# Remainders of the first mixer by VectorE, buffers of transposing streams in turn, and token weights at one byte offset, in a two-layer decoder kernel

## The chip, the cores and the metric

One core of a Trainium2 chip runs the kernel. The metric is device time in microseconds (us) of one execution, as the median of several runs. The engines are named as in the profile: PE is TensorE, PEld its weight loads, DVE is VectorE, ACT is ScalarE, POOL is GpSimd, SP is SyncE, which issues DMAs.

## The reference, cut to what matters

The kernel computes two decoder layers for 256 tokens of 1024 float32 channels, with a root-mean-square norm before each part and at the end. Layer 0 mixes with a gated delta rule (8 heads of 64) beside a short gated convolution; layer 1 with sparse attention. Each layer has a squared-ReLU MLP of 4096 hidden channels.

```python
def reference(x, ...):
    for layer in range(DEPTH):
        h = rms_norm(x, mix_norm[layer])
        if layer % 2 == 0:
            x = x + gdn_shortconv_mixer(h, ...)
        else:
            x = x + nsa_mixer(h, ...)
        x = x + squared_relu_mlp(rms_norm(x, mlp_norm[layer]), w_up[layer], w_down[layer])
    return rms_norm(x, final_norm)

def gdn_shortconv_mixer(h, ...):
    qkv, z, a, b, b_gate, c_gate, hs = jnp.split(h @ w_in, ..., axis=-1)
    qkv = jax.nn.silu(causal_dwconv(qkv, qkv_conv))
    g = -jnp.exp(a_log) * jax.nn.softplus(a + dt_bias)
    o = gated_delta_rule_chunked(l2_normalize(q), l2_normalize(k), v, g, jax.nn.sigmoid(b))
    o = rms_norm(o, o_norm) * jax.nn.silu(z)
    y_b = b_gate * causal_dwconv(c_gate * hs, sc_conv)
    return jnp.concatenate([o, y_b], axis=-1) @ w_out
```

The delta rule solves unit lower-triangular systems of 64 x 64 for every chunk of 64 tokens and every head.

## The kernel before, in words

**Weights in units.** All weights lie in one DRAM tensor, `wts`. SP loads them in pieces of 512 KB into eight staging slots, `st` (128 partitions x 1024 float32), as slots come free. Each 128 x 1024 piece is a *unit*, with a running number `i`. `splits` (L508) makes two halves of each unit: `uh`, which ACT writes as a rounded copy, and the remainder `ul = st - uh`. Four buffers of each hold them in turn (`uh0` to `uh3`, `ul0` to `ul3`). The remainder is made in one of two ways. For most units DVE subtracts (`V.tensor_sub`). For units in the tuple `BYDMA` (L37) ACT writes -uh into `ul`, and `refill` (L529) has POOL issue a DMA that adds `st` to it.

**Products.** A projection multiplies each block by `mm256`, three PE matmuls: high weights by high activations (`xh`), high weights by low activations (`xl`), and remainder by high activations. So PE needs a unit's `uh` for two matmuls and its `ul` for the third. Where activations stand still and weights move, in the projections of one result per token (`proj_tok` and `proj_tok2`, units of 528 and 560 columns instead of 1024), a unit's two halves of 264 or 280 columns are taken one after the other out of `uh` and `ul`.

**What the units are.** 0 to 7 the first projection (k), 8 to 15 the per-token projection of z, a and b (528 columns), 16 to 19 v, 20 to 23 q, 24 to 27 the gate Cg, 28 to 31 h and 32 to 35 Bg of the convolution, 36 to 43 the output projection of the mixer (its products of `yb`, the convolution's result, come before those of `ya`, the delta rule's), 44 to 107 the first MLP. Layer 1 has 108 to 139 (120 to 127 the second per-token projection, 560 columns) and its MLP 140 to 203.

**The first mixer.** `layer0` (L993) computes beside the projections the norms of k and q (`lsq`, which PE sums over partitions by a matmul with `par`), the decay (`g`), the products of keys in a chunk (`al`), and their triangular inverse in `invert`: eight alternating groups of 64 matmuls of 32 x 32 on PE, `left` from `al` and `tt`, `right` from `uc` and `ys`, with a step of DVE between two of them that makes the next `ys`, or the next `tt` and its transpose `uc`. Then come the chain over the chunks, the output `o`, its four transposes on PE (`par,o`), and `ya`. The short convolution (`prepool`, `cvpool`, `tap`, `CG`) is on DVE and POOL.

**Layer 1.** `combine` spawns four `turn` streams for each pair of heads; each takes a PSUM bank and then one of four buffers `pts`, transposes on PE and copies out.

**What sets the order.** The kernel's parts are Python generators. A planner (class `Order`, L166) keeps the time of every engine by a cost table, and at every `yield` decides which stream issues next: streams wait for flags (`yield 'flag'`), take tokens out of counted stocks (`yield 'take'`, `give`) and have priorities. So the program has a fixed order on each engine, and any changed cost or wait can move instructions of all of them. All are recorded in one helper and show line L329 in the profile; tiles tell them apart.

Of the kernel before, what the change touches and what calls it, by code (L numbers as in the profile page):

```python
# [10 lines left out]
F32 = mybir.dt.float32  # L11
F32R = mybir.dt.float32r
BF16 = mybir.dt.bfloat16
I32 = mybir.dt.int32
AF = mybir.ActivationFunctionType
# [11 lines left out]
UN = 1024  # L27
# [6 lines left out]
KPOOL, VPOOL, QPOOL, CVB = (), (), (0, 1, 2, 3), {'conv': 4, 'pool': 2}  # L34
TAP = {'V': 290}
CHAIN, EARLY, TOK_FIRST = 0, 16, False
BYDMA, DLAT = (*range(20, 44, 2), *range(113, 121, 2), *range(129, 141, 2)), 4500  # L37
YIELD = (0.0, 0.0, 0.0)
TICK, BUSY = 10240 / 3, 1500.0
FULL, DRAIN, BARE, STAY, LEAVE = (128, 128), 0.0, 0.0, 0.0, 0.0  # L40
# [1 line left out]
MAIN, SPLIT, SHARE, LIMIT, FLOOR, CAP, SPARE = 9, 0.5, 0.5, 300, -1500.0, 4000.0, 1  # L42
# [123 lines left out]
class Order:  # L166
# [21 lines left out]
    def spawn(self, gen, prio=None):  # L188
        c = self.cur
        if prio is None:  # L190
            prio = 1 if c is None or c.prio in (MAIN, SPLIT) else c.prio
        s = Stream(gen, prio, c)
        self.streams.append(s)
        self._next(s, None)
# [11 lines left out]
    def give(self, name):  # L206
        self.tokens[name].append(self._now())
# [174 lines left out]


BANK = ('bank',)
UB, SB, SPARE1 = 4, 8, 0
SLOTS, PTS = 4, 4
SQ0, NA0 = 'A', dict(V=334)
# [22 lines left out]
def _build(ctx, nc, tc, wts, xin, parin, out, off):  # L410
    e = Ctx()
    order = e.order = Order(8)
    V, A, PE, G = e.eng = [Timed(order, n, x) for n, x in (('V', nc.vector), ('A', nc.scalar), ('PE', nc.tensor),
                                                           ('G', nc.gpsimd))]
# [5 lines left out]
    unitp = pool("unit")  # L420
# [90 lines left out]
    def splits(first):  # L511
        for i in range(first, len(units), 2):
            p, o, n = units[i]
            order.cur.prio = 0 if i < EARLY else SPLIT
            if i >= UB:
                yield 'flag', f'ud{i - UB}'
            yield 'flag', f'ld{p}'
            src = staged[p][:, o:o + n]

            hi = unitp.tile([128, UN + 64], F32R, name=f"uh{i % UB}", tag=f"uh{i % UB}")[:, 32:32 + UN]  # L520
            lo = unitp.tile([128, UN + 64], F32R, name=f"ul{i % UB}")[:, :UN]
            yield 'A'
            A.activation(hi[:, :n], src, AF.Copy)
            made[i] = hi, lo
            if i in BYDMA:
                yield 'A'
                A.activation(lo[:, :n], hi[:, :n].bitcast(F32), AF.Copy, scale=-1.0)
                spawn(refill(i, lo[:, :n], src), SPLIT)
            else:  # L529
                yield 'V'  # L530
                V.tensor_sub(lo[:, :n], src, hi[:, :n].bitcast(F32))
                split_done(i)

    def refill(i, lo, src):
        yield 'G'
        G.dma_start(lo.bitcast(F32), src, accum_op=OP.add)
        order.later(DLAT)
        split_done(i)
# [120 lines left out]
    def proj_tok(norm, half, finish, prio=None):  # L659

        accs = yield from banks(4)
        for k in range(KT):
            hi, lo = yield from unit()
            yield 'flag', f'n{norm.idx}x{k}'
            for t in range(2):
                xt = norm.x[:, k, :, t * 128:t * 128 + 128]
                for b in range(2):
                    if b % GT == 0:
                        yield 'PE'
                    s = slice(b * half, b * half + half)  # L670
                    mm256(accs[2 * t + b][:, :half], xt[:, 0], xt[:, 1], hi[:, s], lo[:, s], k == 0, k == KT - 1)
        spawn(finish(accs), prio)

    def proj_tok2(norm, half, finish):

        for b in range(2):
            accs = yield from banks(2)
            for k in range(KT):
                if k % 2 == 0:
                    hi, lo = yield from unit()  # L680
                yield 'flag', f'n{norm.idx}x{k}'
                s = slice(k % 2 * half, k % 2 * half + half)
                for t in range(2):
                    yield 'PE'
                    xt = norm.x[:, k, :, t * 128:t * 128 + 128]
                    mm256(accs[t][:, :half], xt[:, 0], xt[:, 1], hi[:, s], lo[:, s], k == 0, k == KT - 1)
            spawn(finish(accs, b))
# [878 lines left out]
def layer1(e, n, nxt):  # L1566
# [4 lines left out]
    with ExitStack() as ctx:  # L1571
# [368 lines left out]
        def combine(i, p, PX):  # L1940
            u = 2 * i + p
            yield 'flag', f'pw{u}.0'
            if not MERGE:
                ob = yield BANK
                O = ob[:, :T]
            turns, spreads, ts4 = [4], [2], {}
            for b in range(2):
                yield 'flag', f'pw{u}.{b}'
                tss = ts4[b] = [None, None]
                for s in range(2):  # L1950
                    spawn(turn(u, b, s, PX, tss, turns), TURN)
                if not MERGE:
                    spawn(spread(i, p, b, tss, O, spreads))
            if MERGE:
                for b in range(2):
                    for s in range(2):
                        yield 'flag', f'ts{u}.{b}{s}'
                ob = yield BANK
                O = ob[:, :T]
                yield SMALL  # L1960
                for b in range(2):
                    products(p, b, ts4[b], O, not b)
            else:
                yield 'flag', f'pv{u}'
            yield 'flag', 'cmp1'
            yield 'flag', f'pct{i}'
            yield 'PE'
            pct, left = pcts[i]
            if CL:
                x = pct.rearrange("p a t q -> p a (t q)")  # L1970
                e.mm256(O, *VCB2[p], x[:, 0], x[:, 1], False, True)
            else:
                PE.matmul(O, VCB2[p], pct.rearrange("p t q -> p (t q)"), start=False, stop=True)
            left[0] -= 1
            if not left[0]:
                give('pct')
            if ohl[i] is None:
                ohl[i] = p1.tile([128, 2, 2, T], F32R, name=f"ohl{i}", tag=f"ohl{i}")
            yield from hilo(ohl[i][:, 0, p], ohl[i][:, 1, p], O)
            release(ob)  # L1980
            flag(f'o{u}')

        def turn(u, b, s, PX, tss, left):
            tb = yield BANK
            tp = tb[:, :384]
            yield 'take', 'pts', PTS
            yield 'PE'
            e.keep(tb)
            PE.transpose(tp[:, :128], PX[0][:, s, b], ident)
            PE.transpose(tp[:, 128:256], PX[1][:, s, b, :128], ident)  # L1990
            PE.transpose(tp[:, 256:], PX[1][:, s, b, 128:], ident)
            left[0] -= 1
            if not left[0]:
                give(f'slot{u % SLOTS}')
            ts = p2.tile([128, 384], F32, name="pts", tag="pts", bufs=PTS)
            yield from copy(ts, tp, 'V' if s else 'A')
            release(tb)
            tss[s] = ts
            flag(f'ts{u}.{b}{s}')
# [83 lines left out]
```

## Time and profile before

| | |
|---|---|
| time, median of 3 runs | 672.96 us (672.41 to 673.91) |
| time of the profiled execution | 674.54 us |
| its span | 672.7 us |
| mean granted TensorE clock | 0.988 |
| busy PE, DVE, ACT, POOL | 97%, 68%, 58%, 20% of the span |
| DMA, mean | 179 GB/s |

The profile is of one execution. Its span reaches from the first instruction to the last; the execution's own time is 1.8 us longer. PE's busy share is an average over stages: in the first mixer and in the attention PE waits, in the MLPs it does not. The granted clock is a share of full speed: 1.00 is the upper of two levels (2.4 GHz), 0.50 the lower (1.2 GHz).

### The profile page before, as it was taken

Reading aid. Unit: us, or ns where it says so; the run is one execution under the profiler, and the core shown is the slowest. Engines: PE = TensorE matmul, PEld = TensorE weight load, DVE = VectorE, ACT = ScalarE, POOL = GpSimd, SP = SyncE. Lnnn points to the kernel's source line nnn. Section 1 sums busy time; section 2 is a strip of 40 time slices with the busy share of each in tenths; the row PEclk is TensorE's granted clock in tenths of the full one; section 3 lists DMA queues with packets and bytes.
Section 4 is the critical chain, followed back from the end, with each engine's and each line's share of the span. In section 5 each row is a group of like instructions: output and inputs, shape, how many; then the busy total and the mean of one; then the engine's idle time right before and its main releaser. Section 6 shows DMA issues by size and latency. Waiting matters only on the chain.

```text
span 672.7 us, 16231 instructions
## 1 busy us (share of the span) xinstructions
PE 650.2 (97%) x6642; PEld 623.5 (93%) x6644; DVE 460.4 (68%) x899; ACT 387.7 (58%) x727; POOL 134.4 (20%) x179
## 2 busy tenths in 40 slices
PE   8999789999999999999999999999999999999995
PEld 5999679988999999999999886898999999999995
DVE  6998445865887776555566898897678777644441
ACT  7577234445676665434446679898567666434430
POOL 1012765611300000012024352120220000012121
PEclk9999789999999999999999999999999999999999
DMA  8884654556666666666666748653555555555401
GB/s 293 301 211 157 174 147 120 140 150 154 222 186 190 193 192 196 198 193 190 193 189 160 223 158 291 185 128 89 170 206 188 189 195 200 197 191 189 158 1 63
DMA packets 35642, 120.62 MB, mean 179 GB/s; under 512 B 4080, under 2 KB 4592, under 8 KB 35568
## 3 DMA queue, kind: packets, MB, share of 16 engines
q1 hardware_dynamic: 32112, 107.66, 49.1%
q0 software_dynamic: 3168, 11.54, 9.0%
q8 instruction: 52, 0.85, 0.5%
q10 hardware_dynamic: 288, 0.39, 0.2%
q14 instruction: 22, 0.18, 0.1%
HBM read 106.99 MB, written 1.05 MB: 161 GB/s over the span
## 4 chain that ended last, share of the span: by engine, by line
PE 80%; DVE 9%; ACT 4%; issue 3%; DMA 2%; SPq 0%; DVEq 0%; ACTq 0%
PE b L329 80%; DVE ul L329 2%; ACT uh L329 1%; DMA ul<-st 1%; DMA X<-xt 1%; DMA st<-wts 1%; DVE cvconv L329 1%; DVE rqt L329 1%; ACT E L329 1%; ACT ul L329 1%; DVE al L329 1%; DVE lc L329 0%; DVE u L329 0%; DVE tt L329 0%; DVE nacc L329 0%
## 5 line engine op out<-in xcount | busy, mean ns | idle before, releaser
L329 ACT ACTIVATE uh<-st 128x1024 fp32r<-128x1024 f32 (+3 forms) x204 | 206.2, 1012 | 218.4 <-PE b L329 187.5
L329 PE MATMUL b<-x,uh 128*128 128x256 f32 x1664 | 295.6, 282 | 2.0 <-ACT uh L329 1.8
L329 DVE TENSOR_TENSOR ul<-st,uh 128x1024 fp32r<-128x1024 f32 (+3 forms) x182 | 213.9, 1177 | 119.2 <-ACT uh L329 118.9
L329 PEld LDWEIGHTS b<-x,uh 128*128 128x128 f32 x1664 | 254.2, 190 | 4.1 <-ACT uh L329 1.7
L329 PE MATMUL b<-x,ul 128*128 128x256 f32 x832 | 233.1, 280 | 2.5 <-DVE ul L329 1.3
L329 PE MATMUL b<-U,uh 128*128 128x256 f32 x1024 | 174.2, 276 | 0.0
L329 PEld LDWEIGHTS b<-x,ul 128*128 128x128 f32 x832 | 158.2, 190 | 4.0 <-DVE ul L329 2.6
L329 PEld LDWEIGHTS b<-U,uh 128*128 128x128 f32 x1024 | 154.1, 188 | 0.0
L329 PE MATMUL b<-U,ul 128*128 128x256 f32 x512 | 141.3, 276 | 0.0
L329 PEld LDWEIGHTS b<-U,ul 128*128 128x128 f32 x512 | 96.1, 188 | 0.0
L329 POOL TENSOR_TENSOR nacc<-nacc,sq 128x256 f32<-128x256 f32 x24 | 32.4, 1348 | 227.1 <-ACT sq L329 217.4
L329 POOL DMA_DIRECT2D ul<-st x22 | 19.3, 876 | 80.4 <-ACT ul L329 36.4
L329 DVE SCALAR_TENSOR_TENSOR t<-b,rbc 128x256 f32<-128x256 f32 x64 | 26.6, 424 | 8.3 <-PE b L329 8.3
L329 ACT ACTIVATE U<-u 128x256 fp32r<-128x256 f32 x64 | 26.8, 419 | 2.0
L329 ACT ACTIVATE px<-b,nm 128x256 f32<-128x256 f32 (+1 forms) x64 | 26.3, 423 | 2.0 <-DVE nm L329 1.7
L329 DVE TENSOR_TENSOR U<-u,U 128x256 fp32r<-128x256 f32 x64 | 26.5, 419 | 0.0
L329 POOL TENSOR_TENSOR X<-X,par 128x256 f32<-128x256 f32 x8 | 5.6, 702 | 100.3 <-ACT nacc L329 91.7
L329 ACT ACTIVATE u<-t 128x256 f32<-128x256 f32 x64 | 25.6, 401 | 0.0
L329 DVE TENSOR_TENSOR X<-X,b 128x256 f32<-128x256 f32 (+1 forms) x28 | 13.9, 514 | 16.1 <-PE b L329 16.1
L329 PE MATMUL b<-uh,x 128*128 128x264 f32 (+1 forms) x128 | 24.5, 288 | 0.0
L329 PE MATMUL b<-ohl,uh 128*128 128x256 f32 x128 | 23.9, 287 | 0.2
L329 ACT ACTIVATE ul<-uh 128x1024 fp32r<-128x1024 f32 x22 | 23.2, 1057 | 0.4
(276 smaller groups left out, 793.9 us busy)
## 6 DMA issues: line engine op xcount, KB each, us to landing
st<-wts SPq DMA_DIRECT2D x188, 512.0 KB, 4.3
ul<-st POOLq DMA_DIRECT2D x22, 512.0 KB, 5.4
st<-wts SPq DMA_DIRECT2D x8, 280.0 KB, 3.2
st<-wts SPq DMA_DIRECT2D x8, 264.0 KB, 5.9
st<-wts SPq DMA_DIRECT2D x8, 256.0 KB, 6.1
X<-xt SPq DMA_DIRECT2D x3, 256.0 KB, 6.1
par<-par SPq DMA_DIRECT2D x1, 525.0 KB, 5.8
out_dram<-X SPq DMA_DIRECT2D x2, 256.0 KB, 2.7
```

The costliest lines, as they stand in the source:

```text
L329: r = f(*a, **k)
```

## The change

It has three parts. `BYDMA` shrinks from 22 units to 12: units 22, 24, ... 42 get their remainder from DVE in place of ACT, POOL and a DMA; unit 18 gets it from ACT, POOL and a DMA in place of DVE; unit 20 and those of layer 1 stay. In `combine` a token, of which there is one, is taken before the four `turn` streams are spawned and given back when the fourth has taken its `pts`; and a `turn` takes `pts` ahead of its bank. The per-token weights of 528 and 560 columns lie with their halves 320 elements apart, from element 16 on, in both `uh` and `ul`: each half begins at byte 64 of 256. Before, the halves of `uh` began at bytes 128 and 160 of 256 (264 columns) or 128 and 224 (280), those of `ul` at 0 and 32 or 0 and 96.

```diff
--- before.py
+++ after.py
@@ -34,7 +34,7 @@
 KPOOL, VPOOL, QPOOL, CVB = (), (), (0, 1, 2, 3), {'conv': 4, 'pool': 2}
 TAP = {'V': 290}
 CHAIN, EARLY, TOK_FIRST = 0, 16, False
-BYDMA, DLAT = (*range(20, 44, 2), *range(113, 121, 2), *range(129, 141, 2)), 4500
+BYDMA, DLAT = (18, 20, *range(113, 121, 2), *range(129, 141, 2)), 4500
 YIELD = (0.0, 0.0, 0.0)
 TICK, BUSY = 10240 / 3, 1500.0
 FULL, DRAIN, BARE, STAY, LEAVE = (128, 128), 0.0, 0.0, 0.0, 0.0
@@ -382,6 +382,7 @@
 
 
 BANK = ('bank',)
+TOK, STEP = (528, 560), 320
 UB, SB, SPARE1 = 4, 8, 0
 SLOTS, PTS = 4, 4
 SQ0, NA0 = 'A', dict(V=334)
@@ -517,18 +518,24 @@
             yield 'flag', f'ld{p}'
             src = staged[p][:, o:o + n]
 
-            hi = unitp.tile([128, UN + 64], F32R, name=f"uh{i % UB}", tag=f"uh{i % UB}")[:, 32:32 + UN]
-            lo = unitp.tile([128, UN + 64], F32R, name=f"ul{i % UB}")[:, :UN]
+            hi = unitp.tile([128, UN + 64], F32R, name=f"uh{i % UB}", tag=f"uh{i % UB}")
+            lo = unitp.tile([128, UN + 64], F32R, name=f"ul{i % UB}")
+            if n in TOK:
+
+                made[i] = parts = [a[:, 16:16 + 2 * STEP] for a in (hi, lo)]
+                hi, lo = (a.rearrange("p (b c) -> p b c", b=2)[:, :, :n // 2] for a in parts)
+                src = src.rearrange("p (b c) -> p b c", b=2)
+            else:
+                made[i] = hi, lo = hi[:, 32:32 + n], lo[:, :n]
             yield 'A'
-            A.activation(hi[:, :n], src, AF.Copy)
-            made[i] = hi, lo
+            A.activation(hi, src, AF.Copy)
             if i in BYDMA:
                 yield 'A'
-                A.activation(lo[:, :n], hi[:, :n].bitcast(F32), AF.Copy, scale=-1.0)
-                spawn(refill(i, lo[:, :n], src), SPLIT)
+                A.activation(lo, hi.bitcast(F32), AF.Copy, scale=-1.0)
+                spawn(refill(i, lo, src), SPLIT)
             else:
                 yield 'V'
-                V.tensor_sub(lo[:, :n], src, hi[:, :n].bitcast(F32))
+                V.tensor_sub(lo, src, hi.bitcast(F32))
                 split_done(i)
 
     def refill(i, lo, src):
@@ -667,7 +674,7 @@
                 for b in range(2):
                     if b % GT == 0:
                         yield 'PE'
-                    s = slice(b * half, b * half + half)
+                    s = slice(b * STEP, b * STEP + half)
                     mm256(accs[2 * t + b][:, :half], xt[:, 0], xt[:, 1], hi[:, s], lo[:, s], k == 0, k == KT - 1)
         spawn(finish(accs), prio)
 
@@ -679,7 +686,7 @@
                 if k % 2 == 0:
                     hi, lo = yield from unit()
                 yield 'flag', f'n{norm.idx}x{k}'
-                s = slice(k % 2 * half, k % 2 * half + half)
+                s = slice(k % 2 * STEP, k % 2 * STEP + half)
                 for t in range(2):
                     yield 'PE'
                     xt = norm.x[:, k, :, t * 128:t * 128 + 128]
@@ -1943,7 +1950,8 @@
             if not MERGE:
                 ob = yield BANK
                 O = ob[:, :T]
-            turns, spreads, ts4 = [4], [2], {}
+            turns, spreads, ts4 = [4, 4], [2], {}
+            yield 'take', 'turns', 1
             for b in range(2):
                 yield 'flag', f'pw{u}.{b}'
                 tss = ts4[b] = [None, None]
@@ -1981,9 +1989,12 @@
             flag(f'o{u}')
 
         def turn(u, b, s, PX, tss, left):
+            yield 'take', 'pts', PTS
+            left[1] -= 1
+            if not left[1]:
+                give('turns')
             tb = yield BANK
             tp = tb[:, :384]
-            yield 'take', 'pts', PTS
             yield 'PE'
             e.keep(tb)
             PE.transpose(tp[:, :128], PX[0][:, s, b], ident)
```

The planner then writes another order in the first mixer. PE has the same 5762 matmul instructions in both orders.

ACT, where the v projection begins; `uh2` and `ul2` here are of unit 18, `uh3` of unit 19, `uh0` of unit 20. Before:

```order
L329 ACTIVATE uh2_552<-st_420 128x1024
L329 ACTIVATE K_89<-cvconv_509 128x256
L329 ACTIVATE uh3_581<-st_440 128x1024
L329 ACTIVATE lsq_602<-K_89 128x256
L329 ACTIVATE uh0_611<-st_462 128x1024
L329 ACTIVATE ul0_612<-uh0_611 128x1024
```

and now:

```order
L329 ACTIVATE uh2_552<-st_420 128x1024
L329 ACTIVATE K_89<-cvconv_509 128x256
L329 ACTIVATE ul2_553<-uh2_552 128x1024
L329 ACTIVATE uh3_582<-st_440 128x1024
L329 ACTIVATE lsq_616<-K_89 128x256
L329 ACTIVATE gz0_604<-b7_368,ncol_333 128x256
```

The negation `ul2` of unit 18 stands ahead of the copy of unit 19, and unit 20's copy and negation come later.

DVE, in the triangular inverse, from the first transpose `uc1` to the first `ys`. Before:

```order
L329 STREAM_TRANSPOSE uc1_990<-tt1_988 128x256
L329 TENSOR_TENSOR bv1_1051<-b2_895,beta_98 128x512
L329 TENSOR_TENSOR prepool0_106<-b5_849,rbc_375 128x256
L329 TENSOR_TENSOR prepool1_107<-b0_931,rbc_375 128x256
L329 TENSOR_TENSOR ul3_1056<-st_644,uh3_1055 128x1024
L329 TENSOR_TENSOR ys0_929<-b7_1053,par_75 128x256
L329 TENSOR_TENSOR ys1_991<-b1_1054,par_75 128x256
```

and now:

```order
L329 STREAM_TRANSPOSE uc1_966<-tt1_964 128x256
L329 TENSOR_TENSOR ul2_997<-st_682,uh2_996 128x1024
L329 TENSOR_TENSOR ul1_952<-st_591,uh1_951 128x1024
L329 SCALAR_TENSOR_TENSOR cvconv_968<-preconv0_104,par_75,cvconv_968 128x256
L329 TENSOR_TENSOR preconv1_105<-b2_834,rbc_375 128x256
L329 SCALAR_TENSOR_TENSOR cvconv_968<-preconv0_104,par_75,cvconv_968 128x256
L329 TENSOR_TENSOR ys0_850<-b5_1012,par_75 128x256
L329 TENSOR_TENSOR ys1_967<-b7_1013,par_75 128x256
```

Two subtractions (units 26 and 25) and steps of the convolution of q, k and v (`preconv`, `cvconv`) stand where one subtraction, a product by `beta_98` and the short convolution's first products stood.

PE, in the output projection, around the four transposes of `o`. Before:

```order
L329 MATMUL b_2391<-yb_2136,uh_2392 128x256
L329 MATMUL b_2391<-yb_2137,uh_2392 128x256
L329 MATMUL b_2391<-yb_2136,ul_2393 128x256
L329 MATMUL b_2556<-par,o_2424 128x128 x4
L329 MATMUL b_2388<-ya_2351,uh_2456 128x256
L329 MATMUL b_2388<-ya_2352,uh_2456 128x256
L329 MATMUL b_2388<-ya_2351,ul_2457 128x256
L329 MATMUL b_2388<-ya_2351,uh_2456 128x256
```

and now:

```order
L329 MATMUL b_2410<-yb_2173,uh_2357 128x256
L329 MATMUL b_2410<-yb_2174,uh_2357 128x256
L329 MATMUL b_2410<-yb_2173,ul_2358 128x256
L329 MATMUL b_2495<-par,o_2354 128x128 x4
L329 MATMUL b_2410<-yb_2173,uh_2357 128x256
L329 MATMUL b_2410<-yb_2174,uh_2357 128x256
```

The transposes stood between the last product of `yb` and the first of `ya`; now they stand after the third matmul of unit 38, with 45 matmuls of `yb` behind them. From the end of the first mixer on, the order of every engine is the same in both kernels up to the banks' names.

## Rows read from the trace of the kernel before

**Rows 1.** The page: busy time by engine, and one of the DMA queues.

```profile
PE 650.2 (97%) x6642; PEld 623.5 (93%) x6644; DVE 460.4 (68%) x899; ACT 387.7 (58%) x727; POOL 134.4 (20%) x179
...
q8 instruction: 52, 0.85, 0.5%
```

**Rows 2.** Stretches: length, busy PE, PEld, DVE, ACT, POOL (instructions), clock, DMA share, GB/s.

```profile
72.40:76.70 4.30, 0.22 (x27) 0.12 (x14) 0.86 (x2) 0.00 (x0) 3.99 (x7) 0.90 0.85 228
76.70:82.60 5.90, 5.88 (x138) 5.59 (x141) 1.17 (x3) 2.42 (x3) 3.08 (x5) 0.50 0.33 95
93.20:96.30 3.10, 1.61 (x131) 1.45 (x131) 0.64 (x2) 0.53 (x2) 2.38 (x4) 1.00 0.90 174
96.30:103.10 6.80, 5.72 (x28) 5.63 (x28) 2.63 (x5) 1.98 (x4) 0.00 (x0) 0.50 0.51 152
110.60:173.00 62.40, 60.45 (x722) 57.12 (x717) 43.51 (x100) 29.44 (x43) 19.41 (x26) 1.00 0.60 161
185.00:340.00 155.00, 155.00 (x1369) 155.00 (x1369) 102.59 (x151) 85.40 (x129) 8.93 (x6) 1.00 0.64 193
```

**Rows 3.** PE's timeline, 75 to 100 us: start, length, work, [idle before, releaser].

```profile
76.72 0.87 PE L329 MATMUL b<-ys,uc 32*32 32x32 f32 x49 [4.10 <-issue]
...
86.44 0.95 PE L329 MATMUL b<-ys,uc 32*32 32x32 f32 x85 [0.35 <-issue]
...
94.89 1.25 PE L329 MATMUL b<-ys,uc 32*32 32x32 f32 x122 [1.49 <-issue]
...
98.61 0.59 PE L329 MATMUL b<-x,uh 128*128 128x256 f32 x2 [1.08 <-ACT uh L329]
```

**Rows 4.** Stretches from the start to two of those waits, for their counts.

```profile
0.00:72.60 72.60, 68.12 (x730) 62.11 (x731) 62.50 (x163) 47.05 (x93) 13.39 (x24) 1.00 0.77 239
0.00:94.50 94.50, 84.47 (x1241) 77.42 (x1242) 70.62 (x180) 53.48 (x101) 31.69 (x50) 0.96 0.72 219
```

**Rows 5.** DMA queues, 69 to 74.3 us: packets, MB, share of 16 engines.

```profile
q0 software_dynamic: 114, 0.46, 43.9%
```

**Rows 6.** DMA queues, 74.3 to 76 us.

```profile
q8 instruction: 1, 0.02, 3.5%
```

**Rows 7.** ACT's timeline at 34 us, and DVE's at 43 us.

```profile
34.47 0.42 ACT L329 ACTIVATE K<-cvconv 128x256 f32<-128x256 f32 x1 [0.89 <-DVE cvconv L329]
...
42.78 0.17 DVE L329 SCALAR_TENSOR_TENSOR g<-sp,ea 128x16 f32<-128x16 f32 x1
```

**Rows 8.** PE's timeline at 57 us.

```profile
56.72 1.68 PE L329 MATMUL b<-par,Vf 128*128 128x128 f32 x8 [0.68 <-ACT Vf L329]
```

**Rows 9.** Tile ul, 30 to 185 us: ns min/median/max, first and last start.

```profile
L329 DVE TENSOR_TENSOR ul<-st,uh x23: 1214/1226/1762, 32.5 to 182.9; 128x1024 fp32r<-128x1024 f32 x23
...
L329 POOL DMA_DIRECT2D ul<-st x12: 857/868/1027, 39.0 to 159.5; - x12
...
DMA to landing us min/median/max: 4.4/5.4/9.3
```

**Rows 10.** POOL's timeline, 83 to 88 us.

```profile
83.72 0.61 POOL L329 TENSOR_TENSOR cvpool<-prepool,par 128x256 f32<-128x256 f32 x1
...
86.23 1.60 POOL L329 TENSOR_TENSOR cvpool<-prepool,par 128x256 f32<-128x256 f32 x1
```

**Rows 11.** PE's timeline, 160 to 162 us.

```profile
160.11 0.63 PE L329 MATMUL b<-par,o 128*128 128x128 f32 x4 [0.26 <-DVE o L329]
161.42 0.38 PE L329 MATMUL b<-ya,uh 128*128 128x256 f32 x1 [0.69 <-ACT ya L329]
```

**Rows 12.** PE's timeline at 34 us, and at 386 to 398 us.

```profile
33.76 0.38 PE L329 MATMUL b<-x,ul 128*128 128x256 f32 x1 [0.47 <-DVE ul L329]
...
385.81 0.29 PE L329 MATMUL b<-uh,x 128*128 128x280 f32 x1
...
398.07 0.29 PE L329 MATMUL b<-uh,x 128*128 128x280 f32 x1
```

## The prediction, as it was made before the change was run

> **What bounds the kernel now.** I read the page first: TensorE (PE) is busy for 650.2 of 672.7 us [rows 1]. Next I asked for the busy time of every engine in chosen stretches [rows 2]. In the MLP stretch from 185 to 340 us PE has no idle time at all: 1369 matmuls in 155.0 us, 113.2 ns each. VectorE (DVE) is busy for 102.6 us of it, so an edit to DVE's or ScalarE's (ACT's) work there changes nothing. What can be won lies where PE idles or its clock is down, and that is the first mixer, at 70 to 104 us. In the list of PE's work there [rows 3] four idle times stand among or right behind the 32x32 matmuls of the triangular inverse: 4.10, 0.35, 1.49 and 1.08 us, together 7.02. Three are booked to "issue": PE waited for nothing that the profile shows. In two stretches of 5.90 and 6.80 us the granted clock is 0.50, the lower of the two levels, 1.2 GHz [rows 2]. One follows the idle time of 4.10 us, the other the 1.49. PE was busy in them for 5.88 and 5.72 us; half of that, 5.8 us, is what the clock costs. Idle time and clock together are 12.8 us, nearly all that the mixer has to give.
>
> What are the "issue" waits? The queue q8, whose kind is instruction, carries 52 packets in the run [rows 1]. PE runs 6642 + 6644 = 13,286 matmuls and weight loads: one packet for every 255.5. Counted to the 4.10 us wait they are 730 + 731 = 1461, to the 1.49 us wait 1241 + 1242 = 2483 [rows 4]: 1022 apart, four times 255.5. So PE seems to wait for the next 256 of its instructions. A 32x32 matmul takes about 10 ns (122 in 1.25 us [rows 3]), so two of them and their loads use up a packet 64 times in 1.3 us, where 128x256 matmuls need 14 us. Before the longest wait the queue q0, the GpSimd (POOL) refill of a remainder, takes 43.9% of the DMA engines' time beside the weights' loads [rows 5], and the instruction packet comes only after 74.3 us [rows 6]. PE resumes at 76.72.
>
> By a page of the Trainium skill these waits would be something else: "Runtime: NRT & Kernel Launch", section "Instruction fetch mechanics", has blocks of 256 instructions and fetching that is mostly hidden behind execution. Its block size agrees with 255.5 here; its hiding does not agree with waits that recur at that spacing. By the page alone the change would win nothing at them (second rival).
>
> **The change part by part**, in us against the profiled execution. That one takes 674.54 with a span of 672.7; the median of the runs is 672.96, so 1.58 is taken off at the end.
>
> *A. Unit 18's remainder moves from DVE to ACT, POOL and a DMA.* ACT writes -hi, POOL issues the transfer, and PE's third matmul of the unit waits for it. ACT is free behind K, at 34.47 + 0.42 [rows 7]; the negation takes about as long as a split, so POOL issues at about 36.2. A refill takes 4.4 to 9.3 us, 5.4 in the median [rows 9]: it lands between 40.6 and 45.5. To fill the time the new order puts the norms and the decay's matmul ahead of unit 18. Those need g, which DVE made at 42.78 behind other work [rows 7]; without the subtraction of 1.22 ahead of it I expect it at 41.3, while PE is through with unit 17 at about 39.6. I count 1.5 of new waiting, with 1.1 as the lower end and, for a refill that lands last, 4.7 as the upper. In exchange the transposes of Vf stand later, and their wait of 0.68 [rows 8] goes. **A = +0.8** (0.4 to 4.0).
>
> *B. The remainders of units 22 to 42 move from refills to DVE.* Ten net leave ACT (about 1 us each) and POOL's DMA queue, neither of which bounds PE here; 10 x 1.23 us come to DVE [rows 9]. The waits for instructions stay in number, since PE's list has as many instructions as before, but they fall on other matmuls, and no refill (q0) is under way at the inverse. So I drop the wait of 4.10 to the 1.49 of the next one. Three waits of 1.49 and one of 0.35 make 4.8 in place of 7.02. **B = -2.2** (-4.0, if one more large matmul group covers a fetch, to +2.0, if one of 4.10 stays).
>
> *C. The clock.* The new order spreads the small groups with 12 to 24 large matmuls between them, and the longest idle time becomes about 1.8 us, where the first fall of the clock came behind 4.10. The second came behind 1.49 with PE busy for 1.61 of 3.10 us [rows 2], so this is no sure thing. I take both falls as gone: **C = -5.8** (-5.8 to 0).
>
> *D. The tail of the mixer.* Before, the four transposes of o stand between the products of yb and of ya, and PE waits 0.26 and 0.69 us around them [rows 11] (and some 0.3 more in the next gap). In the new order 45 yb matmuls stand behind them, 5.1 us at 113.2 ns, enough to cover both waits. **D = -1.0** (-1.0 to 0).
>
> *E. The weights at byte 64.* Behind the first per-token projection PE waits 0.47 us for a remainder [rows 12]: what the projection wins is lost in that wait, and I count nothing. The second runs 96 matmuls of 280 columns, the first at 385.81 and the last at 398.07 us: 95 steps of 129.0 ns. Scaled by 280/256 from 113.2, one would take 123.8. I take the difference as the price of where the weights lie: 96 x 5.2 ns, **E = -0.5** (-1.0, if the first wins as much after all, to 0, if it is no matter of place). The form 128x2x264 of the splits moves as many elements; I cost it at nothing, since DVE and ACT wait for PE there.
>
> *F. The token "turns" and the order of bank and pts.* The order of every engine from the end of the first mixer on is the same but for the banks' names: **0**.
>
> *G. What is late next.* DVE works 43.5 of the 62.4 us from 110.6 to 173 [rows 2]; seven subtractions more make it 52. DVE takes its instructions in order: a subtraction that waits for ACT's split holds the steps of the inverse behind it, and the third matmul of a unit waits for DVE. I count one subtraction uncovered, 1.23, and 0.3 for collisions: **G = +1.5** (0 to +6). That a collision costs is seen on POOL: the same product takes 0.61 us alone and 1.60 beside a subtraction [rows 10]; the subtraction itself takes 1226 ns in the median and 1762 at most [rows 9].
>
> "SBUF — State Buffer" of the Trainium skill, section "SBUF: two separate sides", gives the reason: an operation of DVE with two SBUF inputs and one of GpSimd lock each other out of one pair of ports. The trace agrees with the 1.60 us. It speaks against this change, which puts ten more such operations beside POOL's convolution.
>
> Sum: 0.8 - 2.2 - 5.8 - 1.0 - 0.5 + 1.5 = **-7.2**, so 667.3 for the profiled execution and **665.8** against the median.
>
> **The rivals.**
> 1. *One half-clock stretch stays*, behind one of the waits of 1.5 us, as one did before. Half of 5.8 comes back: 668.7. For: the second fall of before. Against: nothing else in the new order is as bare as 72.4 to 76.7. 0.22.
> 2. *The waits are not those for instructions*, or as long as before, and B and C are nothing: -7.2 + 8.0 = +0.8, 673.8. The page on the runtime would have it so; the spacing of 1022 speaks against it. 0.10.
> 3. *Slower: DVE's queue.* Eight subtractions now stand in the hops between the inverse's steps. If each holds the chain for half its time and more, 8 x 0.6 = 4.9, the longer hops also keep the clock down (C = 0): 0.8 - 2.2 - 1.0 - 0.5 + 4.9 = +2.0, 675.0. It decides once the subtractions hold the chain for over 4.3 us together. For: DVE's order after the first uc has two subtractions ahead of ys where it had one. Against: even with 52 us of work DVE keeps 10 us of idle time in the stretch. 0.12.
> 4. *Unit 18's refill lands last*, at 45.5: A is +4.0, 669.0. Against: the median refill takes 5.4 us. 0.06.
>
> **How the numbers follow.** The forecast has 0.50; its own range is 661.6 to 668.5. The range reaches down to A at +0.4, B at -4.0, E at -1.0 and G at 0 (-11.4, 661.6) and up to the second rival (673.8); the third is left out above. A measurement of this kernel tells about 0.2%, 1.35 us, from no change. Below 671.6 lie the forecast and the rivals 1 and 4, 0.78, less 0.02 for their tails; the second makes "same", with a part of those tails, 0.11; the third "slower", 0.13.
>
> **What would show it.** Right: no idle time over 2 us on PE between 70 and 104 us; granted clock 1.00 in all of it; PE waits of about 1.5 us near 40 us; no wait on either side of the transposes of o. If packets of q8 land without PE idling, or the waits stand at another spacing than 255.5, the reading of B is wrong; if the clock falls behind waits of 1.5 us, C is; if DVE's subtractions end PE's waits in the inverse, the third rival has it.

## The result, and the profile after

| | before | changed |
|---|---|---|
| time, median of 6 runs | 673.43 us (672.41 to 677.92) | 668.80 us (668.31 to 669.85) |
| time of the profiled execution | 674.54 us | 668.94 us |
| mean granted TensorE clock in it | 0.988 | 0.993 |

The ratio is 0.992, with a 95% interval of 0.9891 to 0.995. The changed kernel is 4.6 us faster by the medians and 5.6 by the profiled executions, where 7.2 were forecast. (Two comparisons that each took the kernel before again gave medians for it of 673.7 and 673.4, a third 674.8, with runs from 670 to 680: it spreads more than the changed one.)

A group of the triangular inverse, 64 matmuls in the program, stands in the profile as 128; counts such as "the last 108" below are the profile's. "Issue" behind an idle time means that PE waited for nothing that the profile shows.

The page of the changed kernel, busy time and the instruction queue, which answer to [rows 1]:

```profile
PE 647.3 (97%) x6642; PEld 620.9 (93%) x6644; DVE 471.6 (71%) x909; ACT 376.7 (56%) x717; POOL 130.3 (20%) x169
...
q8 instruction: 52, 0.85, 0.5%
```

DVE has ten instructions more, ACT and POOL ten fewer, PE the same number; the 52 packets of instructions are the same, too. Stretches of the changed kernel, with the columns of [rows 2]:

```profile
43.10:50.00 6.90, 6.13 (x26) 5.80 (x27) 3.95 (x15) 0.61 (x4) 0.00 (x0) 0.51 0.78 194
72.00:106.00 34.00, 29.00 (x1052) 27.16 (x1050) 27.58 (x54) 9.03 (x14) 28.00 (x35) 1.00 0.43 125
104.60:173.00 68.40, 68.33 (x797) 65.75 (x796) 53.45 (x111) 30.64 (x48) 20.88 (x26) 1.00 0.38 115
185.00:340.00 155.00, 155.00 (x1370) 155.00 (x1369) 100.67 (x140) 84.68 (x126) 10.08 (x6) 1.00 0.65 195
```

The clock is full through the whole inverse (second row), where it was halved twice. From 104.6 to 173 us PE idles 0.07 us; DVE's 53 us there hold nothing up. The MLP is as it was. But the first row is new: behind 43 us the granted clock is 0.51, with PE busy for 6.13 us. PE's timeline of the changed kernel shows what stands ahead of it, and what is left of the waits in the inverse, [rows 3]:

```profile
40.87 0.61 PE L329 MATMUL b<-par,lsq 128*128 128x2 f32 x4 [0.33 <-ACT lsq L329]
...
43.87 0.58 PE L329 MATMUL b<-x,ul 128*128 128x256 f32 x1 [1.57 <-DMA ul<-st]
...
73.96 1.59 PE L329 MATMUL b<-ys,uc 32*32 32x32 f32 x128 [0.65 <-DVE ys L329]
...
90.88 1.14 PE L329 MATMUL b<-ys,uc 32*32 32x32 f32 x108 [1.05 <-issue]
...
98.33 0.25 PE L329 MATMUL b<-tt,al 32*32 32x32 f32 x4 [1.89 <-issue]
...
103.16 0.38 PE L329 MATMUL b<-ys,uc 32*32 32x32 f32 x22 [1.23 <-issue]
```

At 43.87 PE has waited 1.57 us for unit 18's refill, the one that the change adds, and the clock falls during that wait. Three waits for "issue" are left, together 4.17. ACT's timeline and tile `ul` from 30 to 60 us say when that refill could come:

```profile
35.20 1.05 ACT L329 ACTIVATE ul<-uh 128x1024 fp32r<-128x1024 f32 x1
...
DMA to landing us min/median/max: 5.2/6.2/7.3
```

The negation ends at 36.25, POOL issues at 36.6 and the refill lands 7.3 later, at 43.9. The DMA engines are full: the share is 1.04 from 39.6 to 43.1 us. In the same timeline, the transposes of `o`, [rows 11], have no wait ahead of them or behind. Before, the first four had one, too, of 0.44 us, and the gap behind the last four was followed by another of 0.34:

```profile
141.37 0.66 PE L329 MATMUL b<-par,o 128*128 128x128 f32 x4 [0.44 <-DVE o L329]
...
162.15 0.39 PE L329 MATMUL b<-ya,uh 128*128 128x256 f32 x1 [0.34 <-DVE ya L329]
```

and now:

```profile
138.01 0.66 PE L329 MATMUL b<-par,o 128*128 128x128 f32 x4
150.92 0.63 PE L329 MATMUL b<-par,o 128*128 128x128 f32 x4
```

### The profile page after: what moved, and what is told of

Its sections match the earlier page's. It is cut to its first block, busy times and chain, and to the rows that moved or that the text cites. A ratio compares the mean times of both kernels' runs of the same rounds, so it can differ in the third digit from the quotient of the medians.

```text
span 667.2 us, 16208 instructions
## 1 busy us (share of the span) xinstructions
PE 647.3 (97%) x6642; PEld 620.9 (93%) x6644; DVE 471.6 (71%) x909; ACT 376.7 (56%) x717; POOL 130.3 (20%) x169
## 4 chain that ended last, share of the span: by engine, by line
PE 84%; DVE 6%; DMA 3%; issue 3%; ACT 3%; SPq 0%; DVEq 0%; POOLq 0%; ACTq 0%
PE b L329 84%; DMA ul<-st 2%; DVE ul L329 2%; DMA X<-xt 1%; ACT uh L329 1%; DMA st<-wts 1%; ACT ul L329 1%; DVE kc L329 1%; ACT KD L329 0%; DVE nacc L329 0%; SPq L483 0%; DVE nm L329 0%; DVE kst L329 0%; DVE swq L329 0%; DVE KL L329 0%
## 5 line engine op out<-in xcount | busy, mean ns | idle before, releaser
L329 DVE TENSOR_TENSOR ul<-st,uh 128x1024 fp32r<-128x1024 f32 (+3 forms) x192 | 227.1, 1185 | 118.8 <-ACT uh L329 118.3
L329 POOL DMA_DIRECT2D ul<-st x12 | 10.6, 884 | 58.5 <-DVE K L329 17.8
L329 PEld LDWEIGHTS b<-uh,x 128*128 128x128 f32 x128 | 20.2, 188 | 0.3 <-issue 0.3
```

The lines of the kernel that those rows point to most:

```text
L329: r = f(*a, **k)
```

## The experiments

Each run's ratio is to the kernel before, taken again beside it on the same chip. The runs are called e1 to e11: e1 to e4 shared a chip, then e5 to e8, then e9 to e11. What is said of idle times and the clock is read from one profiled execution of each.

**One part alone.** The new list of units in the kernel before (e1):

```diff
-BYDMA, DLAT = (*range(20, 44, 2), *range(113, 121, 2), *range(129, 141, 2)), 4500
+BYDMA, DLAT = (18, 20, *range(113, 121, 2), *range(129, 141, 2)), 4500
```

> The kernel before with the new list of units (BYDMA) alone: no token for the turns, the per-token weights where they were. Its PE and POOL orders are those of the changed kernel. Theory: the whole gain comes from these units, so 669.0 us (ratio to before 0.992 to 0.995), with the clock's fall near 43 us and the PE waits near 91, 98 and 103 us as in the changed kernel. Rival: where the per-token weights lie is worth 1.5 us or more, then 670.3 us or above.

Measured: 670.49 us, ratio 0.9933 (0.9909 to 0.9958). PE waited 1.87 us for unit 18's refill, and 0.90 and 1.62 in the inverse ahead of the same last 108 and last 4 matmuls as in the changed kernel; the third wait that was expected, near 103 us, did not come. So the list of units makes nearly all of the change: its ratio is 0.9933 where the whole change has 0.992. The time is at the rival's bound, but the ratio lies within what the theory gave.

One thing differs. PE's timeline of e1, and a stretch of it:

```profile
98.16 0.25 PE L329 MATMUL b<-tt,al 32*32 32x32 f32 x4 [1.62 <-issue]
```

```profile
98.00:102.00 4.00, 3.84 (x22) 3.80 (x21) 1.16 (x4) 0.00 (x0) 2.67 (x4) 0.57 0.46 133
```

Behind 1.62 us of waiting the clock falls, to 0.57 over these 4 us. In the changed kernel it stayed at 1.00 behind 1.89 us ahead of the same four matmuls. With one order of PE, the inverse keeps its full clock in one execution and not in another.

Only the weights at byte 64, the third part of the diff, in the kernel before (e2):

> The kernel before with the per-token weights at byte 64 of 256 alone. Theory: worth little, since PE waits for a remainder behind the first of these projections and the second shows steps of 129 ns before and after: 672.7 to 673.4 us (ratio 0.998 to 1.001). Rival: worth 1.5 us or more, 671.9 us or below (ratio 0.998 or less), with 280-column steps at 124 ns.

Measured: 673.10 us, ratio 0.9977 (0.9951 to 1.0002): not told apart from no change. The time lies in the theory's range and the ratio just below it, at the rival's bound; the trace decides. PE's timeline of this run, the first and the last of the 96 matmuls of 280 columns:

```profile
384.25 0.29 PE L329 MATMUL b<-uh,x 128*128 128x280 f32 x1
...
396.39 0.29 PE L329 MATMUL b<-uh,x 128*128 128x280 f32 x1
```

95 steps in 12.14 us are 127.8 ns each, where [rows 12] gave 129.0: 0.1 us in all. The first projection's steps of 264 columns went from 123.2 to 120.9 ns, 0.2 us. But behind the first projection PE waits 0.68 us for a remainder, here and in the changed kernel, where [rows 12] had 0.47, so those 0.2 us are lost again. The place of the weights is worth about 0.1 us, and the 123.8 ns of the forecast were not reached. The waits of the inverse stand where they stood before, ahead of the last 49 and the last 122 matmuls of their groups, but last 3.58 and 2.33 us, where [rows 3] has 4.10 and 1.49: with one order the places repeat and the lengths do not.

The second part of the diff left out of the changed kernel (e8):

> The changed kernel without the token for the turns and with bank ahead of pts as before. The orders of all engines are the same as in the changed kernel, so both theories expect its time, 668.3 to 669.9 us; it is also the control for the other runs of this call.

Measured: 669.25 us, ratio 0.9928 (0.9903 to 0.9953), the changed kernel's time. No effect of the token shows.

**What pulls the clock down at 43 us.** Zeros for PE where it would wait for unit 18's refill, in `proj_m` of the changed kernel (e3):

```diff
                 if k % GM == 0:
                     yield 'PE'
+                if k == 0 and taken[0] == 19:
+                    for _ in range(7):
+                        nc.tensor.matmul(acc, e.zeros[:, :128], e.zeros, start=True, stop=True)
```

> The changed kernel with seven 128x512 matmuls of zeros ahead of unit 18's first matmul, where PE would wait for the refill anyway; every other instruction in the same order. Theory: the clock falls at 43 us because PE stands idle for the refill (0.33 and 1.57 us); with PE kept busy the granted clock stays 1.00 from 43 to 50 us and half of the 6.13 us of work there comes back: 665.7 us, 3.1 below the changed kernel. Rival: the clock falls for another reason, or the zeros delay the unit: 668.8 to 670.4 us with 0.50 at 43 to 50 us.

Measured: 667.56 us, ratio 0.9873 (0.9832 to 0.9913). PE's timeline and the stretch behind it in this run:

```profile
41.58 1.67 PE L661 MATMUL b<-zeros 128*128 128x512 bf16 x7
...
43.94 0.38 PE L329 MATMUL b<-x,ul 128*128 128x256 f32 x1 [0.45 <-DMA ul<-st]
```

```profile
43.10:50.00 6.90, 6.45 (x52) 6.07 (x51) 4.63 (x16) 2.94 (x10) 0.00 (x0) 1.00 0.92 246
```

The refill lands when it did, at 43.94 against 43.87; only the idle time was filled, and the granted clock stays 1.00. The first group of the inverse then starts at 67.59 us, 2.81 before the changed kernel's 70.40. The other profiles say the same: in all six that keep the idle time (the changed kernel, e1, e4, e7, e8 and e9, with 1.56 to 2.48 us ahead of this matmul) the clock falls to 0.50 there, for 6.8 us in three and 3.4 us in three, and in the five that have none or have it filled (e3, e5, e6, e10 and e11) it does not. So it is the idle time that costs the clock. In the changed kernel the clock costs more than the wait (half of 6.13, 3.1 us, beside 1.90); where it was down for 3.4 us it costs about 1.7.

How much of this reaches the end is loose. The ratios, 0.9873 and 0.992, differ by 0.0047, 3.2 us, but their intervals overlap; the medians differ by 2.9 us from e1 on the same chip and by 1.7 from e8. The profiled executions differ by 0.5 us only: the fourteen instructions of the zeros move the waits of the inverse, which are 4.73 us together here where they were 4.17, and 1.7 us more are lost behind the first mixer, where the orders are the same.

Take the refill away instead. In the changed kernel (e5):

```diff
-BYDMA, DLAT = (18, 20, *range(113, 121, 2), *range(129, 141, 2)), 4500
+BYDMA, DLAT = (20, *range(113, 121, 2), *range(129, 141, 2)), 4500
```

> The changed kernel with unit 18's remainder made by DVE again (BYDMA begins with 20); the planner orders the first mixer anew. Theory: unit 18's refill costs the changed kernel the PE waits of 1.57 and 0.33 us and the clock's fall at 43 us (3.1); without it they go and the wait ahead of Vf (0.7) may come back: 664.5 to 666.5 us, granted clock 1.00 from 40 to 60 us. Rival: DVE's further subtraction ahead of g and the inverse costs as much as the refill did: 668 to 671 us.

Measured: 665.10 us, ratio 0.9868 (0.9836 to 0.99), 4.1 below e8 beside it. One stretch of this run:

```profile
39.60:50.00 10.40, 10.40 (x90) 10.22 (x89) 9.63 (x37) 7.04 (x21) 0.07 (x1) 1.00 0.73 212
```

PE has no idle time from 39.6 to 50 us and its full clock. Without the added refill, and in the order that the planner writes then, the kernel is about 4 us faster. The refill is not all that costs: in that order PE waits 1.96 us for DVE between 110 and 173 us, where the changed kernel has no such wait, and in this execution the clock is down from 88.9 to 95.7 us, around waits of 1.13 and 1.87 us.

And unit 20 by DVE as well, so that the list begins with 113 (e6):

> As e5, and unit 20's remainder by DVE too: no refill in the first mixer. Theory: PE is bound by instructions and the clock here and not by DVE: within 1 us of e5. Rival (DVE's queue): each further subtraction shows on the chain, 1.2 us or more above e5.

Measured: 667.82 us, ratio 0.9906 (0.9875 to 0.9936): 2.7 above e5, more than the 1 us that the theory allowed. But in its trace PE waits for DVE only 0.70 us more in the inverse (1.10 in place of 0.65 ahead of the first ys group, and 0.25 ahead of 87.22 us), and the profiled executions of e5 and e6 differ by 0.06 us (667.14 and 667.08). The mean clock of e6's runs is 0.991 or 0.992 in four of six, that of e5's 0.993 to 0.998. This points to the clock for more of the difference than to DVE's queue, but what pulls it down more often was not tried.

**Are the "issue" waits those for the next 256 instructions?** In the changed kernel, the zeros at the start in quarters (e4):

```diff
-            PE.matmul(b, w[:, :128], w, start=True, stop=True)
+            for h in range(4):
+                nc.tensor.matmul(b[:, :128], w[:, :128], w[:, :128], start=True, stop=True)
+            order.spend('PE', *PE.cost('matmul', (b, w[:, :128], w), dict(start=True, stop=True)))
```

> The changed kernel with the eleven matmuls of zeros at the start cut into quarters (128 columns each), the same columns in all: 66 more instructions ahead of everything else on PE, the order otherwise the same. Theory (PE waits for its next 256 instructions): the waits of the inverse move to other matmuls, 33 small ones earlier. With 3.75 us as the shortest time from one block's start to the next I work out 0.3 us near 74.5, 2.4 near 88.4, 0.9 near 93.6 and 0.2 near 102, together 3.8 to 4.1, and none ahead of the last 4 matmuls of a tt group or the last 22 of a ys group, where 1.89 and 1.23 stood; time within 1 us of the changed kernel. Rival (the waits come from other engines, from semaphores or from DMA traffic): they stay before the same matmuls (the last 108, 4 and 22 of their groups).

Measured: 669.16 us, ratio 0.9901 (0.9865 to 0.9937). PE's timeline:

```profile
85.12 0.27 PE L329 MATMUL b<-x,ul 128*128 128x256 f32 x1 [0.56 <-issue]
...
89.12 0.18 PE L329 MATMUL b<-tt,al 32*32 32x32 f32 x1 [2.50 <-issue]
...
98.77 0.52 PE L329 MATMUL b<-tt,al 32*32 32x32 f32 x37 [1.34 <-issue]
...
104.14 0.67 PE L329 MATMUL b<-ys,uc 32*32 32x32 f32 x55 [0.29 <-issue]
```

66 more instructions at 1.2 us, 33 matmuls with their loads, and 90 us later the waits stand exactly 33 matmuls earlier: ahead of the last 37 where it was the last 4, ahead of the last 55 where it was the last 22, and ahead of the last 1 of a tt group with 12 large matmuls and the 128 of a ys group behind it, 141, where it was the last 108. The place of the wait belongs to the count of instructions and not to the work. The lengths came out as expected at two places (2.50 for 2.4, 0.29 for 0.2) and not at the others: 1.34 stood where 0.9 was expected, and 0.56 at 85.12 us in place of 0.3 near 74.5. Around the waits of 2.50 and 1.34 us the clock fell.

The same was tried to make the waits small, on the kernel of e5. One matmul of zeros instead of eleven (`if not j:` ahead of it; e10):

> The kernel of e5 with one matmul of zeros at the start in place of eleven: 20 instructions fewer ahead of everything else on PE, the order otherwise the same. Theory: the blocks of 256 instructions end 10 small matmuls later; with 3.75 us as the shortest time from block to block I work out waits of 0.3, 0.3 and 1.0 us (near 71.5, 83 and 90), 1.6 together where e5 showed 1.13 and 1.87, and no fall of the clock behind them: 662.5 to 664.5 us. Rival: the zeros at the start are needed for the clock of the first projection, which loses 1 to 3 us: 665 to 668 us.

Measured: 664.86 us, ratio 0.9841 (0.9809 to 0.9873), between the two theories. The waits were 0.16, 0.52 and 1.83 us, 2.5 together, and around the last the clock fell, which the theory had excluded. And 126 small ones (e11):

```diff
-            PE.matmul(b, w[:, :128], w, start=True, stop=True)
+            for _ in range(11 + (j < 5)):
+                nc.tensor.matmul(b[:, :44], w[:, :128], w[:, :44], start=True, stop=True)
+            order.spend('PE', *PE.cost('matmul', (b, w[:, :128], w), dict(start=True, stop=True)))
```

> The kernel of e5 with 126 matmuls of 44 columns of zeros at the start in place of eleven of 512: 230 instructions more, so that the blocks end 13 small matmuls later than in e5 (256 - 230 = 26 instructions). Theory: waits of 0.3, 0.3, 0.3 and 0.5 us, together 1.5, none over 0.6, no fall of the clock in the inverse; the start is 1 to 2 us longer, since 126 such matmuls take 6 to 7 us where eleven took 4.7: 664 to 666 us with PE's waits in the inverse 1.5 below e5's. Rival (the waits are not those for instructions): 1.1 and 1.9 us stay where they stood.

Measured: 664.42 us, ratio 0.984 (0.9807 to 0.9872), within the theory's range, and the clock did not fall in the inverse. PE's timelines of e5, e10 and e11 at the same place:

```profile
87.35 0.39 PE L329 MATMUL b<-x,ul 128*128 128x256 f32 x1 [1.13 <-issue]
...
88.02 1.47 PE L329 MATMUL b<-ys,uc 32*32 32x32 f32 x124
91.35 0.32 PE L329 MATMUL b<-ys,uc 32*32 32x32 f32 x4 [1.87 <-issue]
```

```profile
87.47 1.50 PE L329 MATMUL b<-ys,uc 32*32 32x32 f32 x128
88.91 0.50 PE L329 MATMUL b<-x,uh 128*128 128x256 f32 x2
89.25 0.28 PE L329 MATMUL b<-x,ul 128*128 128x256 f32 x1
89.37 0.41 PE L329 MATMUL b<-x,uh 128*128 128x256 f32 x2
89.61 0.28 PE L329 MATMUL b<-x,ul 128*128 128x256 f32 x1
91.72 0.58 PE L329 MATMUL b<-x,uh 128*128 128x256 f32 x1 [1.83 <-issue]
```

```profile
87.16 1.31 PE L329 MATMUL b<-ys,uc 32*32 32x32 f32 x128
88.40 0.50 PE L329 MATMUL b<-x,uh 128*128 128x256 f32 x2
88.74 0.28 PE L329 MATMUL b<-x,ul 128*128 128x256 f32 x1
88.85 0.40 PE L329 MATMUL b<-x,uh 128*128 128x256 f32 x2
89.09 0.28 PE L329 MATMUL b<-x,ul 128*128 128x256 f32 x1
89.21 0.40 PE L329 MATMUL b<-x,uh 128*128 128x256 f32 x2
89.44 0.28 PE L329 MATMUL b<-x,ul 128*128 128x256 f32 x1
90.90 0.50 PE L329 MATMUL b<-x,uh 128*128 128x256 f32 x2 [1.17 <-issue]
...
94.63 0.28 PE L329 MATMUL b<-tt,al 32*32 32x32 f32 x9 [1.27 <-issue]
```

The wait moved from the last 4 of the ys group to behind six large matmuls (10 later, as 20 instructions should make it) and behind nine (13 later, as 26 should). Its length did not follow: e11 waits 0.80, 1.17 and 1.27 us, 3.2 in place of the 1.5 worked out and twice over the 0.6 that none should pass, e10 2.5 in place of 1.6; e5 had 1.13 and 1.87. Two waits that are one block of 256 instructions apart end 4.00 us apart in e4 (85.12 and 89.12) and in e5 (87.35 and 91.35) and 3.73 in e11 (90.90 and 94.63). So 3.75 us is near the shortest time from block to block, but it is a rough number. The intervals of e5, e10 and e11 lie below that of e8, which has the changed kernel's order; among the three they overlap.

**Why the wait of 4.10 us was so long.** More transfers in POOL's queue, behind the subtractions of units 26 and 27 of the changed kernel (e7):

```diff
                 V.tensor_sub(lo, src, hi.bitcast(F32))
+                if i in (26, 27):
+                    for h in range(2):
+                        nc.gpsimd.dma_start(e.scrap, src[:, h * 512:h * 512 + 512])
```

> The changed kernel with four more transfers of 256 KB in POOL's queue behind the subtractions of units 26 and 27, near 71 us, into a buffer that nobody reads; the orders of PE, DVE, ACT and SP are the same. Theory: the 4.10 us wait of before was so long because a refill and the weights' loads kept the DMA engines full while PE's next instructions had to come; so a wait of 1 to 3 us appears at the next block's start near 71 to 75 us, where the changed kernel shows 0.65 or less, the clock may fall behind it, and the time is 670 to 674 us. Rival: the long wait came of the position alone: 0.5 us or less there and the time within 1 us of the changed kernel.

Measured: 670.13 us, ratio 0.9943 (0.9922 to 0.9965), 0.9 above e8 with overlapping intervals, and no wait ahead of the last 27. This run tells nothing of the question: the transfers waited for each other, the last was issued at 69.89 and landed 2.9 us later, before the first ys group began at 73.58. Better aimed, unit 26 by a refill again, in the changed kernel, with PE's order as it is (e9):

```diff
-BYDMA, DLAT = (18, 20, *range(113, 121, 2), *range(129, 141, 2)), 4500
+BYDMA, DLAT = (18, 20, 26, *range(113, 121, 2), *range(129, 141, 2)), 4500
```

> The changed kernel with unit 26's remainder by a refill again (BYDMA begins 18, 20, 26); PE's order stays as it is, DVE does one subtraction fewer, ACT and POOL's queue one copy and one refill more. Theory: this refill is what made the wait of 4.10 us of before so long, by keeping the DMA engines full while PE's next instructions had to come; the wait ahead of the last 27 matmuls of the first ys group (0.1 to 0.4 us in the changed kernel) becomes 1.5 to 4 us, the clock falls behind it, and the time is 671 to 675 us. Rival: its length came of where the block's end lay; 0.5 us or less there, and the time within 1.2 us of the changed kernel.

Measured: 670.42 us, ratio 0.9927 (0.9903 to 0.9952): by the ratio the changed kernel's time. PE's timeline:

```profile
76.73 0.44 PE L329 MATMUL b<-ys,uc 32*32 32x32 f32 x27 [1.17 <-issue]
...
86.68 0.87 PE L329 MATMUL b<-ys,uc 32*32 32x32 f32 x76 [1.73 <-issue]
```

The wait ahead of the last 27 is 1.17 us, where the changed kernel's profile lists none and e8's 0.38, and one of 1.73 stands in the next ys group, where neither has one; the clock does not fall behind them. All its waits for instructions in the inverse are 6.4 us together, where the other four profiles with this order of PE (the changed kernel, e1, e7 and e8) have 2.5 to 5.1. That agrees with a refill beside the inverse lengthening the waits, but one execution does not show it, and no wait came near 4.10. What else held the packet back in the kernel before (more loads under way, or where its block ended) stays open.

## Why the prediction was right, and where not

The time lies within the range, and it is faster, as forecast. But the range reached up to the second rival's 673.8; the forecast's own range ended at 668.5, 0.3 us below the 668.8 measured, and the gain is two thirds of the forecast's by the medians. (The 0.2% that the prediction took as what a measurement tells from no change was too small: the interval here reaches 0.3% to either side.) The time is the first rival's number (668.7), and that is luck: one stretch at half clock stays, but at 43 us, behind unit 18's refill, where the rival had it in the inverse. By the prediction's steps, on the profiled executions:

- **A, unit 18, was mis-sized: +0.8 forecast, about +4.3 measured.** The new waiting is 0.33 + 1.57 = 1.90 against the 1.5 taken, and the 0.68 ahead of Vf went, as said. What failed is that the step stopped at the wait. PE's clock was halved behind it, which costs half of 6.13, 3.1 us; the rule that step C used for the inverse (an idle stretch pulls the clock down behind itself) was not applied to the idle time that the change itself made. e3 shows that the idle time was the cause, e5 that all of it goes with the refill. The wait was also not for what the step had in mind: DVE made g at 41.12 us, where 41.3 was forecast, and PE did not wait for it but for the refill, which took 7.3 us where the median of 5.4 was taken. The DMA engines were full then; that this is why it took so long was not tested.
- **B, the waits from 70 to 104 us: -2.2 forecast, -2.9 measured** (7.02 to 4.17). Of the 7.02, the 1.08 was for ACT's `uh` and is gone; the waits for instructions went from 5.94 to 4.17, -1.8, where the step took 4.8 for them, -1.1. The places of these waits are shown to follow the count of instructions by e4, e10 and e11, to the very matmul. The page "Runtime: NRT & Kernel Launch" of the Trainium skill, section "Instruction fetch mechanics", has the blocks of 256 instructions right, as these shifts show; that crossing a block's end is mostly hidden holds in the MLP (155.00 of 155.00 us busy) and not in the inverse. The lengths were not foreseen: executions with the changed kernel's order have 2.5 to 5.1 us together, so that B came out near its forecast is in part luck. The reason given for the 4.10, the refill of unit 26, is not shown (e9).
- **C, the clock in the inverse: -5.8, as forecast, in this execution.** Both falls are gone; 1.00 from 72 to 106 us. The step called it no sure thing, and it is none: in e1, with the same order of PE, 1.62 us of waiting brought the clock down for 3.4 us, of which half, 1.7 us, is lost, and in e7 1.50 us did the same.
- **D, the tail: -1.0 forecast, -1.7 measured**: the waits of 0.26, 0.69 and 0.34 us are all gone, and so is the 0.44 ahead of the first four transposes, which the step did not count.
- **E, the place of the weights: -0.5 forecast, -0.1 measured** by the steps of e2. What the first projection won was lost in the wait behind it, as the step said; the price of 5.2 ns a matmul was too high, 1.3 came back.
- **F, the token: 0**, as forecast (e8).
- **G, DVE: +1.5 forecast, +0.4 measured**: the wait ahead of the first ys group went from 0.26 to 0.65 us, and no other wait for a subtraction came up in the inverse. The collisions on which the step and the argument against the change rested did come: six products of POOL took 1.52 to 1.65 us beside subtractions there, where 0.61 is usual. But no wait of PE ended on POOL, so they cost nothing. The third rival, the slower one, did not happen.

Together: 4.3 - 2.9 - 5.8 - 1.7 - 0.1 + 0.4 = -5.8. The changed execution also reached its first wait behind the per-token projection 0.4 us later than the other (34.17 against 33.76 us), which no step covers; with it -5.4, where the two profiled executions differ by -5.6.

What the signs in the prediction said: "PE waits of about 1.5 us near 40 us" and "no wait on either side of the transposes of o" came true; "no idle time over 2 us" and "granted clock 1.00" between 70 and 104 us, too. "If the clock falls behind waits of 1.5 us" happened as well, at 43 us, outside the stretch that C was about, and in e1 inside it. And "if packets of q8 land without PE idling" was no good sign: 52 land in each execution and PE idles at three of them.

## What to carry to other kernels

When a change makes PE wait somewhere, price the clock behind the wait as well: here 1.9 us of waiting cost 3.1 more, and filling the idle time with work that nobody needs kept the clock up. Waits of 1.5 to 1.9 us in the inverse brought the clock down in some executions and not in others, so one profile does not tell what an order is worth. Where a stretch has many very short instructions, count them: the waits for instructions come at a fixed count, whatever the work. A shift of the count moved them (4.2 us together became 4.7 in e4) and did not remove them; more large matmuls between the short ones were not tried by themselves. For a transfer added on the critical path, look at the DMA load of that very moment beside the median over the run: here 7.3 us stood against 5.4.

## What the runs showed that was not expected

126 matmuls of 44 columns of zeros at the start, with their loads, took 4.20 us, 33 ns each, about what the eleven of 512 columns took that they replaced (3.98 us in the kernel before, 4.69 in the changed one); I had expected 6 to 7. And with one such matmul instead of eleven, PE idled 3.43 us ahead of its first product and the kernel lost nothing that shows (664.86 us, ratio 0.9841, against 665.10 and 0.9868 of e5).
